# A two-layer transformer pair on one core: the low halves of the mixing stage's split weights, formed by VectorE or by accumulating DMAs

## The chip, the cores and the metric

The kernel runs on one core of a Trainium2 chip. The metric is device time in microseconds (us) of one execution. Before the change three runs took 1903.65, 1903.70 and 1907.62 us, a median of 1903.7 us.

## The reference

256 rows of 1024 numbers pass through a first network of two layers, then a second of two layers. A layer of the first network is

```python
mod = silu(c) @ ada_w[l] + ada_b[l]                      # nine vectors: shift, scale, gate x 3
h = h + 0.5 * g1 * swiglu(modulate(rms_norm(h), sh1, sc1), ffn1_w_in[l], ffn1_w_out[l])
z = modulate(rms_norm(h), sh2, sc2) @ w_in[l]            # 1024 -> 2564 columns: the mixing part
mixed = concat(diff_attention(z), conformer_conv(z), spatial_gating(z), forgetting_attention(z))
h = h + g2 * (mixed @ w_out[l])
h = h + 0.5 * g3 * swiglu(modulate(rms_norm(h), sh3, sc3), ffn2_w_in[l], ffn2_w_out[l])
```

The convolution is causal and depthwise, 31 taps wide. The second network (attention with three kinds of heads, then an MLP) is not touched by the change.

## The kernel before

**Split products.** Most products are made at full precision from float32r operands, which hold fewer bits than float32. A weight tile `raw` is split into `hi`, its rounded copy, and `lo = raw - hi`; the rows on the other side are split alike. A product is then three matmuls: rows hi by weight hi, rows hi by weight lo, rows lo by weight hi. In `pump` (line 413) ScalarE (ACT) writes `hi` by a copy that rounds (a CAST in the trace) and VectorE (DVE) writes `lo` by a subtraction:

```python
sc_.copy(hi[:, :n], raw[:, :n])
ve.tensor_tensor(lo[:, :n], raw[:, :n], hi[:, :n].bitcast(F), op=OP.subtract)
```

Weights come in chunks of at most 128 x 1024 numbers (512 KB). `fetch` (line 395) loads them through SyncE's queue (SP), in the order of a list `stream`; `pump` makes the splits when its plan finds buffers and time; `chunk` (line 452) hands them to the matmul loops. All large tiles come from one ring of 40 buffers.

**The mixing part** (`mixing`, line 1069) multiplies by `w_in` in six blocks of columns (`MIX_BLOCKS`), each made of four chunks, over two halves of the rows, tt0 and tt1. Blocks 0, 1, 2 and 4 are split: 16 chunks a layer, twelve of 128 x 1024 and the four of block 1 of 128 x 520. I number them 0 to 15 in the order of use. Blocks 3 and 5 and all of `w_out` stay whole (float32, no split). `gemm_in` (line 791) runs over blocks and halves; where the rows of tt1 are not ready it takes block 0 tt0, block 1 tt0, block 0 tt1, block 1 tt1. Block 0 feeds the convolution, whose 31 taps for two column halves run on DVE (`conv`, line 1113), block 1 and 2 the forgetting attention, 3 and 5 the differential attention, 4 the spatial gating.

**Rows.** Before the mixing part `Normed` (line 597) takes each half's sum of squares on ACT (two `junk` instructions, one for each 512 columns), the reciprocal root on GpSimd (POOL), scales the rows on DVE, and `to_xT` (line 700) transposes them on TensorE (PE) into two banks, applies the modulation (the first bank on ACT, the second on DVE; `c<-bank,mod,mod` in the trace) and splits them. The residual sums of the stage before (`ev<-bank,c`, then `h<-h,ev`) are on DVE.

**Order.** Python code records every instruction while it keeps a plan of each engine's clock from costs of its own (`Plan`, `Engine.cost`). Work that isn't a matmul of the main loops is a generator that is stepped when that plan says that it is due. So each engine's program is one fixed sequence, in the order in which the plan met the work, and it waits in that order on the chip. All compute instructions are issued by one helper, line 183, so tiles tell the work apart: `c` is a tile of the ring, `bank` a PSUM bank, `ev`, `sm`, `dl`, `st` smaller tiles.

Of the kernel before, what the change touches and what calls it, by code (L numbers as in the profile page):

```python
# [7 lines left out]
F = mybir.dt.float32  # L8
R = mybir.dt.float32r
AF = mybir.ActivationFunctionType  # L10
OP = mybir.AluOpType
AX = mybir.AxisListType

P = 128
# [12 lines left out]
MIX_BLOCKS = [[(768, 512)], [(2304, 260)], [(1792, 512)], [(0, 512)], [(1280, 512)], [(512, 256)]]  # L27
# [8 lines left out]
def width(block):  # L36
    return sum(n for _, n in block)


def in_sizes(blocks):  # L40
    return [2 * width(b) for b in blocks for _ in range(4)]


def out_sizes(k):
    return [1024] * (k // P)
# [197 lines left out]
def two_blocks(ctx: ExitStack, tc, w, out, dbg=None, stages=99):  # L243
    nc = tc.nc
    pool = ctx.enter_context(tc.tile_pool(name="sb", bufs=1))
# [9 lines left out]
    WHOLE = (3, 5)  # L255
    plan = Plan()
    pe, ve, sc_, gp = (Engine(plan, k, e) for k, e in (("pe", nc.tensor), ("dve", nc.vector), ("act", nc.scalar), ("pool", nc.gpsimd)))
# [36 lines left out]
    def wait(cond, what):  # L294
        n = 0
        while not cond():
            pump()
            if not bg.tick():
                bg.idle()
            flush()  # L300
            n += 1
            assert n < 20000, (what, st, arena.free, psr.free, mine, smr.free, dlr.free, evr.free, describe())
# [11 lines left out]
    def drain(entries):  # L314
        n = 0
        while True:
            left = [e for e in entries if e[2] is not None]
            if not left:
                return
            pump()  # L320
            moved = bg.tick()
            for e in left:
                if e[2] is bg.rest and e not in bg.rest[: bg.width] and e[1] <= plan.now:
                    moved += bg.step(e)
            if not moved:
                bg.idle()
            flush()
            n += 1
            assert n < 20000, (st, plan.clock, arena.free, psr.free, mine, smr.free, dlr.free, evr.free, describe(), [e[1] for e in bg.urgent + bg.rest])


    units = []

    def add(nm, l, sizes, whole=lambda i: False):
        at = 0
        for i, n in enumerate(sizes):
            units.append((w[nm][l, at * P:(at + n) * P].rearrange("(p n) -> p n", p=P), n, "whole" if whole(i) else None))
            at += n

    parts = []  # L340
    for l in range(L):
        for i in range(3):
            at = len(units)
            if i == 1:
                add("w_in", l, in_sizes(MIX_BLOCKS), lambda i: i // 4 in WHOLE)
                add("w_out", l, out_sizes(D), lambda i: True)
            else:
                add(f"ffn{i // 2 + 1}_w_in", l, in_sizes(FFN_BLOCKS))
                add(f"ffn{i // 2 + 1}_w_out", l, out_sizes(DFF))
            parts.append(units[at:])  # L350
    units.clear()
    for l in range(L):
        at = len(units)
# [37 lines left out]
    def spare(n=1):  # L391

        return arena.free >= n and (st["held"] + n <= NBASE or arena.free >= n + SPARE)

    def fetch():
        while st["fetch"] < len(stream) and st["raws"] < NRAW and spare():
            ap, n = stream[st["fetch"]][:2]
            t = arena.take([P, 1024])
            nc.sync.dma_start(t[:, :n], ap)
            begin = max(plan.clock["dma"], plan.now)  # L400
            plan.clock["dma"] = begin + n * 1.42e-3
            plan.wrote(t, plan.clock["dma"] + 2.0, "dma")
            raw_of[st["fetch"]] = t
            st["fetch"] += 1
            st["raws"] += 1
            st["held"] += 1

    def next_raw():
        del raw_of[st["conv"]]
        st["conv"] += 1  # L410
        st["raws"] -= 1

    def pump(force=False, most=None, goal=None):
        while True:
            fetch()
            i = st["conv"]
            if i >= st["fetch"] or i == most or st["made"] == goal:
                return
            ap, n, what = stream[i]
            raw = raw_of[i]  # L420
            ahead = st["made"] - st["want"]
            if not force and (st["made"] < 4 * EARLY or plan.ready(raw) > plan.now + 0.3):
                return
            if what == "whole":
                chunks.append((raw, None))
                st["made"] += 1
                next_raw()
                continue
            if what is not None:
                if not ada_unit(raw, *what):  # L430
                    return
                arena.put()
                st["held"] -= 1
                next_raw()
                continue
            if st["made"] - st["released"] >= NMOST or not (spare(2) or (force and ahead <= 0 and arena.free >= 2)):
                return
            if not force and st["hurry"] and ahead >= 4:
                return
            late = max(plan.clock["act"], plan.clock["dve"]) - plan.now  # L440
            if not force and late > (0.5 if ahead >= 5 else 2.0 if ahead >= 3 else 4.0):
                return
            hi, lo = arena.take([P, 1024], R), arena.take([P, 1024], R)
            st["held"] += 1
            arena.put()
            sc_.copy(hi[:, :n], raw[:, :n])
            ve.tensor_tensor(lo[:, :n], raw[:, :n], hi[:, :n].bitcast(F), op=OP.subtract)
            chunks.append((hi, lo))
            st["made"] += 1
            next_raw()  # L450

    def chunk():
        i = st["want"]
        n = 0
        while len(chunks) <= i:
            pump(True, goal=min(i + 2, 4 * EARLY) if EARLY <= i < 4 * EARLY else i + 1 if i < EARLY else None)
            if len(chunks) <= i and not bg.tick():
                bg.idle()
            flush()
            n += 1  # L460
            assert n < 20000, (st, arena.free, describe())
        st["want"] += 1
        c = chunks[i]
        chunks[i] = None
        return c
# [75 lines left out]
    def ada_unit(raw, l, v, kt):  # L541
        key = (l, v)
        if v % 3 != 2:
            t = mod_tile(l, v)
            ve.tensor_tensor_reduce(raw, raw, cond_row, scale=1.0, scalar=K("ada_b", 72 * l + 8 * v + kt, 1), op0=OP.mult, op1=OP.add,
                                    accum_out=t[:, kt:kt + 1])
            if kt + 1 in (FIRST if key in ((0, 0), (0, 1)) else [KT]):
                a = slice(mod_there[key], kt + 1)
                if v % 3 == 1:
                    ve.scalar_tensor_tensor(t[:, a], t[:, a], 1.0, K("norm_g", 24 * l + 8 * (v // 3) + a.start, a.stop - a.start),  # L550
                                            op0=OP.add, op1=OP.mult)
                mod_there[key] = a.stop
            return True
        if key not in ada_acc:
            if not room(3):
                return False
            ada_acc[key] = arena.take([P, D]), arena.take([P, D])
            br = ada_acc[key][1]
            nc.sync.dma_start(br[0:1], w["ada_b"][l:l + 1, v * D:(v + 1) * D])
            plan.wrote(br, plan.now + 3.0, "dma")  # L560
        acc, br = ada_acc[key]
        c = cond[:, kt:kt + 1]
        if kt == 0:
            ve.tensor_scalar(acc, raw, c, None, op0=OP.mult)
        else:
            ve.scalar_tensor_tensor(acc, raw, c, acc, op0=OP.mult, op1=OP.add)
        if kt == KT - 1:
            ve.tensor_tensor(acc[0:1], acc[0:1], br[0:1], op=OP.add)
            arena.put()
            bg.add(ada_reduce(l, v, acc), urgent=True, due=plan.ready(acc) + 2.0)  # L570
        return True
# [1073 lines left out]
    at = CON["causal"][0]  # L1645
# [166 lines left out]
```

## Time and profile before

| | |
|---|---|
| runs | 1903.65, 1903.70, 1907.62 us |
| the profiled execution's own time | 1907.24 us |
| its span on the core | 1905.5 us, mean granted TensorE clock 0.996 |
| PE busy | 1864.3 us (98%), 8672 matmuls |
| DVE busy | 1303.6 us (68%), 2044 instructions |
| ACT busy | 972.5 us (51%), 1506 instructions |
| POOL busy | 17.0 us (1%), 56 instructions |
| DMA | 397.32 MB, mean 209 GB/s |

A busy PE is not a PE at its peak: matmuls are pipelined and their ends are modelled. In the rows below a group or a timeline row gives engine, operation, output tile and input tiles, shapes and count; what stands in square brackets is how long the engine sat idle before it and what ended that. PEclk is the granted TensorE clock as a share of full speed. The mixing parts of the two layers lie at about 195 to 330 us and 690 to 825 us of the span.

### The profile page before, as it was taken

How to read it: one execution, taken by the hardware profiler on the slowest of the kernel's cores; microseconds unless marked ns; L12 is line 12 of the kernel's file. 1: busy time of each engine (PE TensorE's matmuls, PEld its weight loads, DVE VectorE, ACT ScalarE, POOL GpSimd, SP SyncE). 2: the span in 40 equal slices, each digit the busy share in tenths (PEclk: the TensorE clock that was granted, in tenths of full speed). 3: DMA queues.
4: the chain of work that ended last, by engine and by line, in shares of the span. 5: the costliest groups of instructions: out<-in, count | busy, mean ns of one | idle time of the engine just before them, and what ended most of it. 6: DMA issues, size and time to landing. Idle time of an engine off the chain costs nothing.

```text
span 1905.5 us, 23848 instructions
## 1 busy us (share of the span) xinstructions
PE 1864.3 (98%) x8672; PEld 1487.9 (78%) x8672; DVE 1303.6 (68%) x2044; ACT 972.5 (51%) x1506; POOL 17.0 (1%) x56
## 2 busy tenths in 40 slices
PE   6999999999999999999999999999999999999998
PEld 5788864888888886668888787888888787888886
DVE  7999796878697967865566646676654546666561
ACT  5544545444454545654445646555543645645460
POOL 0000000000000000000000000000000000000000
PEclk9999999999999999999999999999999999999999
DMA  9989752678688865435565343655574343654460
GB/s 384 382 329 394 259 192 78 234 268 297 246 296 288 334 240 194 156 130 189 192 239 188 111 155 102 215 170 167 180 250 141 125 159 107 197 195 160 146 220 34
DMA packets 110579, 397.32 MB, mean 209 GB/s; under 512 B 12278, under 2 KB 12406, under 8 KB 110460
## 3 DMA queue, kind: packets, MB, share of 16 engines
q1 hardware_dynamic: 109020, 391.88, 59.4%
q10 hardware_dynamic: 1440, 3.91, 0.6%
q8 instruction: 68, 1.11, 0.2%
q14 instruction: 51, 0.42, 0.1%
HBM read 394.69 MB, written 1.05 MB: 208 GB/s over the span
## 4 chain that ended last, share of the span: by engine, by line
PE 87%; DVE 5%; ACT 5%; issue 1%; DMA 1%; POOL 0%; ACTq 0%; POOLq 0%; DVEq 0%
PE bank L183 87%; DVE c L183 3%; ACT sm L183 2%; ACT c L183 2%; DVE sm L183 1%; ACT L175 1%; DMA cond_row<-in_c_dram 0%; DVE ev L183 0%; DMA c<-in_ada_w_dram 0%; DMA c<-in_w_out_b_dram 0%; DVE st L183 0%; DVE h L183 0%; ACT ev L183 0%; ACT junk L183 0%; ACT dl L183 0%
## 5 line engine op out<-in xcount | busy, mean ns | idle before, releaser
L183 PE MATMUL bank<-c,c 128*128 128x512 f32 (+3 forms) x7392 | 1761.9, 396 | 10.9 <-ACT c L183 7.8
L183 PEld LDWEIGHTS bank<-c,c 128*128 128x128 f32 (+1 forms) x7392 | 1350.0, 188 | 327.4 <-issue 45.8
L183 DVE TENSOR_TENSOR c<-c,c 128x1024 fp32r<-128x1024 f32 (+4 forms) x614 | 711.5, 1182 | 233.4 <-ACT c L183 225.4
L183 ACT CAST c<-c 128x1024 fp32r<-128x1024 f32 (+4 forms) x600 | 592.0, 1025 | 112.7 <-PE bank L183 74.7
L183 ACT ACTIVATE ev<-bank 128x256 f32<-128x256 f32 (+1 forms) x100 | 40.0, 401 | 198.4 <-PE bank L183 196.2
L183 DVE CUSTOM_DVE_ANT_0 c<-c,cond_row,col 128x1024 f32<-128x1024 f32 x96 | 121.9, 1275 | 0.0
L183 ACT CAST c<-bank 128x512 fp32r<-128x512 f32 (+1 forms) x100 | 55.2, 553 | 86.5 <-PE bank L183 86.5
L183 DVE TENSOR_TENSOR c<-bank,c 128x512 fp32r<-128x512 f32 (+2 forms) x108 | 69.6, 647 | 24.1 <-ACT c L183 24.1
L183 DVE TENSOR_TENSOR ev<-ev,bank 128x256 f32<-128x256 f32 x88 | 36.4, 417 | 67.4 <-ACT ev L183 67.1
L183 ACT ACTIVATE ev<-bank,st 128x512 f32<-128x512 f32 x56 | 38.5, 688 | 77.6 <-PE bank L183 77.6
L183 ACT ACTIVATE junk<-h 128x512 f32<-128x512 f32 x44 | 27.8, 631 | 95.2 <-DVE h L183 94.8
L183 PEld LDWEIGHTS bank<-con,ev 128*128 128x128 f32 x432 | 55.9, 140 | 25.5 <-issue 4.9
L183 PE MATMUL bank<-con,ev 128*128 128x128 f32 x432 | 72.3, 273 | 3.2 <-DVE ev L183 3.2
L183 ACT CAST c<-ev 128x512 fp32r<-128x512 f32 x28 | 17.4, 620 | 91.4 <-DVE ev L183 91.2
L183 ACT ACTIVATE c<-bank,st 128x512 f32<-128x512 f32 x36 | 24.8, 688 | 75.2 <-PE bank L183 69.7
L183 DVE SCALAR_TENSOR_TENSOR c<-c,cond,c 128x1024 f32<-128x1024 f32 x42 | 53.7, 1278 | 0.0
L183 DVE TENSOR_TENSOR ev<-ev 128x512 f32<-128x512 f32 x32 | 22.1, 690 | 45.5 <-ACT ev L183 45.5
L183 DVE TENSOR_TENSOR ev<-bank,c 128x512 f32<-128x512 f32 x40 | 27.4, 685 | 34.4 <-PE bank L183 34.3
L183 DVE SCALAR_TENSOR_TENSOR c<-c,col,c 128x256 f32<-128x256 f32 x120 | 48.8, 474 | 0.0
L183 ACT ACTIVATE sm<-sm,st 128x128 f32<-128x128 f32 x72 | 31.8, 443 | 17.3 <-DVE st L183 17.3
L183 DVE TENSOR_TENSOR h<-h,bank 128x512 f32<-128x512 f32 x16 | 10.9, 682 | 42.1 <-PE bank L183 42.1
L183 DVE TENSOR_TENSOR c<-ev,c 128x512 fp32r<-128x512 f32 x28 | 19.4, 692 | 23.1 <-ACT c L183 23.0
(106 smaller groups left out, 676.0 us busy)
## 6 DMA issues: line engine op xcount, KB each, us to landing
c<-in_ffn_w_in_dram SPq DMA_DIRECT2D x176, 512.0 KB, 4.8
c<-in_w_in_dram SPq DMA_DIRECT2D x152, 512.0 KB, 4.2
c<-in_ada_w_dram SPq DMA_DIRECT2D x144, 512.0 KB, 5.9
c<-in_ffn_w_out_dram SPq DMA_DIRECT2D x88, 512.0 KB, 5.5
c<-in_w_up_dram SPq DMA_DIRECT2D x64, 512.0 KB, 4.2
c<-in_w_down_dram SPq DMA_DIRECT2D x64, 512.0 KB, 4.3
c<-in_w_out_dram SPq DMA_DIRECT2D x16, 512.0 KB, 4.4
c<-in_w_o_dram SPq DMA_DIRECT2D x16, 512.0 KB, 4.2
```

Of the source, the lines that this page charges most:

```text
L175: self.eng.preload_act_table_set(table)
L183: return fn(*args, **kw)
```

## The change

For the 32 split chunks of the two mixing parts, ACT writes the negated rounded copy into `lo` (an `ACTIVATE` with scale -1 into a float32r tile), a DMA issued by POOL adds `raw` to it where it lies, and ACT then writes `hi` as before. The subtraction on DVE goes. In the plan's books the DMA takes 1 us of POOL, and `lo` is there 6 us later.

```diff
-    def add(nm, l, sizes, whole=lambda i: False):
+    def add(nm, l, sizes, whole=lambda i: False, other=None):
...
-            units.append((w[nm][l, at * P:(at + n) * P].rearrange("(p n) -> p n", p=P), n, "whole" if whole(i) else None))
+            units.append((w[nm][l, at * P:(at + n) * P].rearrange("(p n) -> p n", p=P), n, "whole" if whole(i) else other))
...
-                add("w_in", l, in_sizes(MIX_BLOCKS), lambda i: i // 4 in WHOLE)
+                add("w_in", l, in_sizes(MIX_BLOCKS), lambda i: i // 4 in WHOLE, "added")
...
-            if what is not None:
+            if what not in (None, "added"):
...
+            if what == "added":
+                sc_.activation(lo[:, :n], raw[:, :n], AF.Copy, scale=-1.0)
+                nc.gpsimd.dma_start(lo[:, :n], raw[:, :n], accum_op=OP.add)
+                plan.note("pool", 1.0, [], [lo, raw])
+                plan.wrote(lo, plan.clock["pool"] + 6.0, "dma")
             sc_.copy(hi[:, :n], raw[:, :n])
-            ve.tensor_tensor(lo[:, :n], raw[:, :n], hi[:, :n].bitcast(F), op=OP.subtract)
+            if what is None:
+                ve.tensor_tensor(lo[:, :n], raw[:, :n], hi[:, :n].bitcast(F), op=OP.subtract)
```

The plan's new costs also move other instructions. Three places in layer 0 show it; layer 1 has the same new order in all three.

**ACT, from the squares of the rows of tt1 (`junk`) to the modulation of those rows (`ACTIVATE c<-bank,mod,mod`).** The CASTs from a `c` tile of 128x520 are chunks of block 1, that of 128x1024 is chunk 8, the first of block 2. Before:

```order
L183 ACTIVATE junk_1931,st_1916<-h_66 128x512
L1080 DMA ws<-in_gmlp_ws_dram 128x512
L1082 DMA c_1943<-in_gmlp_rows_dram 128x512
L183 CAST c_1961<-c_1775 128x520
L183 CAST c_1970<-c_1780 128x520
L183 CAST c_1979<-c_1787 128x520
L175 ACT_TABLE_LOAD
L183 ACTIVATE ev_1988<-bank_1945 128x256
L183 CAST c_1997<-c_1795 128x1024
L183 ACTIVATE c_2005<-bank_2006,mod_3_1006,mod_4_790 128x128 x4
```

Now:

```order
L183 CAST c_1959<-c_1766 128x520
L183 ACTIVATE c_1967<-c_1775 128x520
L183 CAST c_1966<-c_1775 128x520
L183 ACTIVATE c_1980<-c_1780 128x520
L183 CAST c_1979<-c_1780 128x520
L175 ACT_TABLE_LOAD
L183 ACTIVATE ev_1989<-bank_1943 128x256
L183 ACTIVATE c_1999<-c_1787 128x520
L183 CAST c_1998<-c_1787 128x520
L183 ACTIVATE c_2006<-c_1796 128x1024
L183 CAST c_2005<-c_1796 128x1024
L183 ACTIVATE c_2014<-bank_2015,mod_3_1006,mod_4_790 128x128 x4
```

Ahead of the second piece stand the same two DMA issues and chunk 4's ACTIVATE. So between the squares and the modulation ACT now has five chunks twice (four of 520, one of 1024), where it had three of 520 and one of 1024 once.

**DVE, from the first taps of the convolution to the scaled rows `dl` of the forgetting attention's tt0.** The taps are `SCALAR_TENSOR_TENSOR` on a `c` tile of 128x256; `st<-ev` is the reduction that `dl` depends on. Before:

```order
L183 TENSOR_SCALAR c_2167<-c_2040,col 128x256 x2
L183 SCALAR_TENSOR_TENSOR c_2167<-c_2040,col,c_2167 128x256 x8
L183 TENSOR_TENSOR ws<-ws,con 128x512
L183 TENSOR_REDUCE st_2206<-ev_2205 128x8
L183 TENSOR_TENSOR c_2222<-c_2001,c_2221 128x1024
L183 SCALAR_TENSOR_TENSOR c_2167<-c_2040,col,c_2167 128x256 x8
L183 TENSOR_TENSOR dl_2203<-bank_2160,st_2242 128x8x64
```

Now:

```order
L183 TENSOR_SCALAR c_2182<-c_2037,col 128x256 x2
L183 SCALAR_TENSOR_TENSOR c_2182<-c_2037,col,c_2182 128x256 x16
L183 TENSOR_TENSOR ws<-ws,con 128x512
L183 TENSOR_REDUCE st_2226<-ev_2225 128x8
L183 SCALAR_TENSOR_TENSOR c_2182<-c_2037,col,c_2182 128x256 x8
L183 TENSOR_TENSOR dl_2223<-bank_2172,st_2250 128x8x64
```

A subtraction of 128x1024 is gone, and 24 taps instead of 16 stand ahead of `dl`.

**PE, the transposes of that `dl` among the matmuls of block 3** (whole weights; `bank_2252` before, `bank_2273` now). Before:

```order
L183 MATMUL bank_2252<-c_1908,c_1867 128x512 x2
L183 MATMUL bank_2252<-c_1965,c_1867 128x512 x2
L183 MATMUL bank_2252<-c_1974,c_1867 128x512
L183 MATMUL bank_2278<-con,dl_2203 65x128 x4
L183 MATMUL bank_2284<-con,dl_2203 65x128 x4
```

Now:

```order
L183 MATMUL bank_2273<-c_1964,c_1871 128x512 x2
L183 MATMUL bank_2290<-con,dl_2223 65x128 x4
L183 MATMUL bank_2296<-con,dl_2223 65x128 x4
L183 MATMUL bank_2273<-c_1971,c_1871 128x512 x2
L183 MATMUL bank_2273<-c_1984,c_1871 128x512 x2
```

The transposes stood behind five matmuls of block 3 and stand behind two. (A float32 matmul of this list is two instructions in the trace.)

## Rows read from the trace of the kernel before

**Rows 1.** The page, parts 1 and 4: busy time of engines; the last chain.

```profile
PE 1864.3 (98%) x8672; PEld 1487.9 (78%) x8672; DVE 1303.6 (68%) x2044; ACT 972.5 (51%) x1506; POOL 17.0 (1%) x56
...
PE 87%; DVE 5%; ACT 5%; issue 1%; DMA 1%; POOL 0%; ACTq 0%; POOLq 0%; DVEq 0%
```

**Rows 2.** Busy time by stretch: length, PE, PEld, DVE, ACT, POOL, PEclk, DMA, GB/s.

```profile
195.00:330.00 135.00, 130.34 (x579) 89.86 (x577) 105.91 (x266) 73.54 (x166) 2.39 (x9) 0.97 0.51 173
690.00:825.00 135.00, 131.25 (x595) 91.47 (x594) 99.61 (x255) 72.99 (x166) 2.44 (x9) 0.99 0.48 160
...
240.00:250.00 10.00, 10.00 (x38) 6.62 (x37) 10.00 (x22) 3.64 (x7) 0.00 (x0) 1.00 0.62 211
```

**Rows 3.** The same view, layer 1, around a wait of PE for block 2.

```profile
736.00:738.00 2.00, 0.50 (x1) 0.19 (x1) 1.23 (x2) 2.00 (x3) 0.00 (x0) 1.00 0.01 2
738.00:740.00 2.00, 1.85 (x5) 1.47 (x6) 2.00 (x5) 0.06 (x1) 0.00 (x0) 0.56 0.00 0
```

**Rows 4.** Groups by form: the subtractions, and an ACTIVATE of 128x1024.

```profile
L183 DVE TENSOR_TENSOR c<-c,c 128x1024 fp32r<-128x1024 f32 x574 | 687.8, 1220 | 228.0 <-ACT c L183 220.6 <-PE bank L183 2.6 <-DMA c<-in_ffn_w_in_dram 2.1
...
L183 ACT ACTIVATE c<-c 128x1024 f32<-128x1024 f32 x12 | 12.0, 1050 | 0.0
...
L183 DVE TENSOR_TENSOR c<-c,c 128x520 fp32r<-128x520 f32 x8 | 5.2, 693 | 0.0
```

**Rows 5.** Timeline (start, us), layer 0: rows of tt0, then tt1, into the mixing part.

```profile
206.05 2.93 ACT L183 CAST c<-c 128x1024 fp32r<-128x1024 f32 x3
...
209.34 1.50 ACT L183 ACTIVATE c<-bank,mod,mod 128x128 f32<-128x128 f32 x4 [0.36 <-PE bank L183]
...
212.14 1.36 DVE L183 TENSOR_SCALAR c<-bank,mod,mod 128x128 f32<-128x128 f32 x4
...
215.41 0.68 DVE L183 TENSOR_TENSOR ev<-bank,c 128x512 f32<-128x512 f32 x1
...
219.15 1.68 ACT L183 CAST c<-c 128x520 fp32r<-128x520 f32 x3 [0.19 <-issue]
...
219.52 0.55 POOL L183 TENSOR_TENSOR st<-st,small 128x1 f32<-128x1 f32 x1
...
220.10 0.76 DVE L183 TENSOR_SCALAR c<-h,st 128x1024 f32<-128x1024 f32 x1 [0.94 <-POOL st L183]
...
223.36 1.51 ACT L183 ACTIVATE c<-bank,mod,mod 128x128 f32<-128x128 f32 x4
...
225.57 8.87 PE L183 MATMUL bank<-c,c 128*128 128x512 f32 x48 [0.54 <-ACT c L183]
```

**Rows 6.** Timeline, layer 0: last copies of block 2, taps, block 2 tt0's end, block 3, `dl`.

```profile
233.49 1.99 ACT L183 CAST c<-c 128x1024 fp32r<-128x1024 f32 x2
...
239.75 3.25 DVE L183 SCALAR_TENSOR_TENSOR c<-c,col,c 128x256 f32<-128x256 f32 x8
240.17 0.60 ACT L183 ACTIVATE ev<-bank 128x512 f32<-128x512 f32 x1 [1.18 <-PE bank L183]
...
245.56 4.54 PE L183 MATMUL bank<-c,c 128*128 128x512 f32 x10
...
249.94 1.04 PE L183 MATMUL bank<-con,dl 128*65 128x128 f32 x8
```

**Rows 7.** Loads of `w_in`: from issue to landing, us.

```profile
DMA to landing us min/median/max: 2.8/4.3/9.0
```

**Rows 8.** Timeline, layer 0: gating reads block 4 tt1; the next stage's first transposes.

```profile
276.31 0.60 ACT L183 ACTIVATE c<-bank 128x512 f32<-128x512 f32 x1 [1.53 <-PE bank L183]
...
330.36 1.06 PE L183 MATMUL bank<-con,c 128*128 128x128 f32 x8
```

**Rows 9.** Timeline, layer 1: copies of block 1; first matmuls after block 4; next transposes.

```profile
716.24 1.69 ACT L183 CAST c<-c 128x520 fp32r<-128x520 f32 x3 [0.18 <-issue]
...
777.09 1.03 PE L183 MATMUL bank<-c,c 128*128 128x256 f32 x4
...
824.35 1.09 PE L183 MATMUL bank<-con,c 128*128 128x128 f32 x8
```

## Prediction, made before the changed kernel ran

> **What bounds the kernel now.** I began with the page's busy times and last chain. TensorE is busy for 98% of the span and holds 87% of the chain that ended last; VectorE, which the change relieves, is busy for 68% and holds 5% [rows 1]. So time taken from VectorE is worth something only where TensorE stands still. The change touches the two mixing parts, so I next read the busy times of those two stretches. TensorE lacks 135 - 130.34 = 4.7 us in layer 0 and 135 - 131.25 = 3.8 us in layer 1, and the granted clock, 0.97 and 0.99, costs some 0.03 x 135 + 0.01 x 135 = 5.4 us more [rows 2]. That is 13.9 us: more than this the change cannot give. The reader should also see that VectorE is full in a stretch such as 240 to 250 us, while TensorE is full there too [rows 2]. Third, the timeline around the places where the weights of the mixing part are split shows which copy each matmul waits for: there ACT, not VectorE, ends TensorE's waits, as at 225.57 us [rows 5].
>
> **What is removed.** 24 subtractions of 1.22 us and 8 of 0.69 us [rows 4], 34.8 us of VectorE, 17.4 us a layer. By the order only those of chunks 12 to 15, 4.9 us a layer, lie among the taps of the convolution; the rest lie before it.
>
> **What is added on ACT.** A negated copy for each chunk. An ACTIVATE of 128x1024 takes 1.05 us [rows 4]; back to back, a copy of 128x1024 costs 2.93 / 3 = 0.98 us and one of 128x520 1.68 / 3 = 0.56 us [rows 5]. The order shows where they queue; I follow layer 0.
>
> Step 1, rows of tt0. Chunks 1 to 3 are copied between the squares and the modulation of tt0. Three more copies let ACT reach the modulation at 206.05 + 6 x 0.98 = 211.9 us instead of 209.34 [rows 5]. VectorE's own modulation stands behind the first bank's subtraction: 211.9 + 1.50 + 0.62 + 0.69 = 214.7 us instead of 212.14. Before, chunk 4's subtraction (0.69) stood between it and the residual sums of tt1; that one is gone. So these start at about 217.4 us instead of 215.41: **+2.0 us**, for all of tt1.
>
> Step 2, rows of tt1. Between squares and modulation ACT now has five more copies of 0.56 us and one of 0.98 us, **+3.8 us**. The modulation moves from 223.36 [rows 5] to 229.2 us, and block 0 tt1 on TensorE, which waited 0.54 us for exactly this chain at 225.57 [rows 5], starts at 231.4 us. Block 1 tt0, the only work put ahead of it, fills little of the gap.
>
> Step 3, block 2. Three more negations (chunks 9 to 11) stand on ACT before the last copy of block 2, which ended at 233.49 + 1.99 = 235.5 us [rows 6]: now 235.5 + 5.8 + 2.9 = 244.2 us, the negation a microsecond earlier, at 243.2. Then the accumulate. No row shows one. The nearest are the loads of as many bytes, 2.8 to 9.0 us from issue to landing [rows 7]. Less than nothing is excluded, since the matmul waits for it. I take the median, 4.3 us: 247.5 us, and 1.1 us of matmuls after it. Block 2 tt0 ends at 248.6 us instead of 240.17 [rows 6], **+8.4 us**.
>
> Step 4, the convolution's place. Its taps start after ACT's copies of step 3: just ahead of the tap row at 239.75 us stand two TENSOR_SCALARs, 0.7 us, so 239.1 + 8.7 = 247.8 us now. Sixteen taps come first, then the mask and the reduction (0.7 us each), eight taps, and the `dl` product: 247.8 + 0.7 + 6.5 + 1.3 + 3.3 + 0.6 = 260.2 us, by the tap row's 3.25 us for eight [rows 6]. TensorE is there at 248.6 + 5.2 (block 2 tt1) + 1.7 (two matmuls of block 3; 4.54 us for five of them [rows 6]) = 255.5 us and waits. It transposed `dl` at 249.94 us [rows 6] with five of those matmuls done, so the loss is 260.3 - 249.9 + 3 x 0.9 = **12.9 us**. The subtraction that stood here is already left out; with it the wait would be 1.2 us longer.
>
> Step 5, what is paid back. From here on VectorE is ahead and TensorE runs on. Block 4 ends at 276.2 + 12.9 = 289.1 us. From its end to the next stage's transposes TensorE took 330.36 - 276.2 = 54.1 us in layer 0 [rows 8], with waits and a low clock, but 824.35 - 777.09 = 47.3 us in layer 1 [rows 9]. With the convolution ready early I give both layers 47. Layer 0: 336.1 us, **+5.8 us**. Layer 1 stands at the same place of ACT's order 716.24 - 219.15 = 497.1 us later [rows 5, 9], and its new order is the same: 289.1 + 497.1 + 47 = 833.2 us against 824.35 [rows 9], **+8.9 us**. It loses more because its old order had less to pay back.
>
> **POOL and SP.** POOL was busy for 17 us [rows 1], so its 32 issues find it free; each waits for its negation, and the reciprocal roots of the rows (one ended at 220.07 us [rows 5]) stand between them in the order. The accumulates that those roots wait behind have their negations done on ACT before the squares, so the roots lose nothing. Loads that reuse a `raw` buffer wait for its accumulate; they are issued far ahead, and I cost that at nothing. If that cover is gone, one landing time a layer is lost.
>
> **Sum.** 5.8 + 8.9 = 14.7 us. The profiled execution's own time is 1907.2 us, so 1921.9 us by it; it lies 3.5 us above the median of the runs, and from that, 1903.7 us, I forecast **1918 us**.
>
> **A page against the rows.** The loads took 2.8 to 9.0 us [rows 7]. The Trainium skill, "DMA: Bandwidth & Descriptors", section "Anatomy of one DMA — SWDGE (gpsimd) path", gives a DMA issued by GpSimd about 2.0 us plus its bytes at 436 GB/s; for 512 KB I work out 3.2 us, an estimate from that page. By it step 3 would be 1.1 us shorter and the sum the same, since step 4 waits for VectorE either way; no row here shows such a DMA.
>
> **The rivals.** (a) *VectorE's relief wins, faster.* All that the mixing parts can give is 13.9 us [rows 2]. For it: VectorE full at 240 to 250 us. It decides if ACT's added copies find idle time, that is, if chunks are split earlier than the order suggests. Against it: the wait at 225.57 us names ACT [rows 5]. Half of it: 1897 us.
>
> (b) *No change.* The delays of steps 1 to 4 are there, and the last third of the stage, where layer 0 lost 54.1 - 47.3 = 6.8 us, pays back more than I give it in both layers: 1906 us.
>
> (c) *Late landing.* The accumulate of chunk 4 is issued after the root of tt1, at 220.1 + 2.0 = 222.1 us, and by the order the transposes of tt1 (1.0 us) stand behind its first use on TensorE. ACT reaches the modulation at 229.2 us, so from 229.2 - 1.0 - 222.1 = 6.1 us of landing on, each further microsecond delays both layers. At 9.0 us: 2 x 2.9 = 5.8 us, 1924 us; an accumulate that reads two operands may need longer, 1930 us at 12 us. VectorE's scaling of the rows follows the same root and holds VectorE for 0.76 us, for 1024 columns in which a subtraction takes 1.22 us [rows 4, 5]. If POOL cannot issue beside it, landings longer than 5.3 us are enough. That is what the Trainium skill's page "SBUF — State Buffer", section "Who interferes with whom", leads one to expect: it says that a VectorE instruction in a two-port mode locks GpSimd out, and that this starves the descriptors of a GpSimd DMA. No row here shows an issue by POOL to weigh it by.
>
> Low clock belongs to all of them: after a slice in which TensorE worked 0.5 of 2 us the grant was 0.56 [rows 3]. The waits of steps 2 to 4 are as long, but most of what then runs slowly waits for ACT anyway; I add nothing, and up to 3 us a layer to the upper end.
>
> **How the numbers follow.** Forecast 0.57, its own range 1911 to 1925; (c) 0.18; (b) 0.14; (a) 0.11. About 0.2%, 3.8 us, is what a measurement can tell from no change. Faster by more: (a), 0.11. Within: (b) but for 0.01, so 0.13. Slower: 0.57 + 0.18 + 0.01 = 0.76. The range of 8 in 10 leaves out (a) and the far end of (c): 1903 to 1931 us.
>
> **What would show it.** Right: block 0 tt1 waits for ACT some 6 us later after the squares than before; a wait of PE on VectorE before the `dl` transposes; VectorE ending the taps before block 4 ends; both stages longer, layer 1 more. Wrong: PE without new waits between 215 and 262 us; accumulates landing after 6 us or more (then c); the last third still taking 54 us.

## The result, and the profile after

The changed kernel took 1934.9 us (median of 4 runs, 1933.2 to 1936.6) beside 1904.0 us for the one before on the same chip: a ratio of 1.0156, 95% interval 1.0142 to 1.0169, so 31 us slower. I had forecast 1918 us, 14 us slower, and a range up to 1931.

The page of the changed kernel: busy times, two DMA queues (packets, MB, share of 16 engines), the last chain, the costliest group.

```profile
PE 1873.8 (97%) x8672; PEld 1498.8 (77%) x8672; DVE 1270.9 (66%) x2010; ACT 1005.1 (52%) x1544; POOL 45.4 (2%) x88
...
q1 hardware_dynamic: 109020, 391.88, 58.0%
q0 software_dynamic: 4608, 14.71, 4.1%
...
PE 88%; ACT 5%; DVE 3%; DMA 3%; issue 1%; POOL 0%; ACTq 0%; POOLq 0%; DVEq 0%
...
L183 PE MATMUL bank<-c,c 128*128 128x512 f32 (+2 forms) x7392 | 1767.3, 397 | 32.3 <-DMA c<-c 23.4
```

Beside [rows 1], VectorE lost 32.7 us, ACT gained as much, and VectorE's share of the chain fell from 5% to 3%. The last line has the new item: TensorE waited 23.4 us for `DMA c<-c`, the accumulates. Their queue, q0, moved 14.71 MB in 4.1% of the engines' time.

Busy time by stretch, the columns of [rows 2]:

```profile
195.00:330.00 135.00, 119.54 (x544) 88.73 (x543) 82.65 (x238) 84.99 (x177) 15.95 (x23) 0.92 0.77 222
690.00:825.00 135.00, 121.65 (x563) 94.68 (x562) 77.19 (x223) 79.22 (x162) 15.86 (x23) 0.94 0.78 226
246.00:256.00 10.00, 3.69 (x14) 2.44 (x15) 7.84 (x21) 2.00 (x5) 0.01 (x1) 1.00 0.95 267
258.00:260.00 2.00, 2.00 (x6) 1.61 (x5) 2.00 (x6) 0.51 (x2) 0.00 (x0) 0.50 0.00 0
```

TensorE lacks 15.5 and 13.4 us instead of 4.7 and 3.8, and the clock fell to 0.92 and 0.94. (Over the whole stages, which now end later, it lacks as much: 15.5 of 150.7 us and 13.4 of 149.5.) Between 246 and 256 us it worked 3.7 of 10 us while the DMA engines were 95% busy, and from 258 to 260 us, behind these waits, the granted clock was 0.50, the lower of its two levels.

TensorE's timeline in layer 0, from the rows of tt1 to the next stage (start, us):

```profile
228.90 0.80 PE L183 MATMUL bank<-c,c 128*128 128x260 f32 x2 [6.20 <-DMA c<-c]
...
246.86 1.65 PE L183 MATMUL bank<-c,c 128*128 128x512 f32 x6 [1.08 <-DMA c<-c]
251.97 1.66 PE L183 MATMUL bank<-c,c 128*128 128x512 f32 x6 [3.46 <-DMA c<-c]
255.62 7.13 PE L183 MATMUL bank<-c,c 128*128 128x512 f32 x23 [1.99 <-DMA c<-c]
...
265.90 1.04 PE L183 MATMUL bank<-con,dl 128*65 128x128 f32 x8
...
295.64 0.60 PE L183 MATMUL bank<-c,c 128*128 128x256 f32 x2
...
300.68 2.24 PE L183 MATMUL bank<-c 32*128 32x256 f32 x14 [1.29 <-DVE c L183]
...
345.71 1.06 PE L183 MATMUL bank<-con,c 128*128 128x128 f32 x8
```

Chunk 4 held TensorE for 6.2 us, the last three chunks of block 2 for 1.1, 3.5 and 2.0. The transposes of `dl`, before which I expected a wait for VectorE, start at 265.90 us with no wait. Block 4 ended at 295.64 us, and the next stage's transposes came 15.4 us later than at 330.36 [rows 8]. ACT's rows that answer to steps 1 to 3 (both modulations, block 2 tt0's end):

```profile
211.93 1.49 ACT L183 ACTIVATE c<-bank,mod,mod 128x128 f32<-128x128 f32 x4
230.59 1.50 ACT L183 ACTIVATE c<-bank,mod,mod 128x128 f32<-128x128 f32 x4 [1.60 <-PE bank L183]
257.08 0.60 ACT L183 ACTIVATE ev<-bank 128x512 f32<-128x512 f32 x1 [8.79 <-PE bank L183]
```

Layer 1, TensorE (the first four answer to the waits above, then block 4's end and the next stage):

```profile
740.61 0.80 PE L183 MATMUL bank<-c,c 128*128 128x260 f32 x2 [5.51 <-DMA c<-c]
...
758.68 1.65 PE L183 MATMUL bank<-c,c 128*128 128x512 f32 x6 [1.19 <-DMA c<-c]
762.46 1.65 PE L183 MATMUL bank<-c,c 128*128 128x512 f32 x6 [2.13 <-DMA c<-c]
...
765.98 5.54 PE L183 MATMUL bank<-c,c 128*128 128x512 f32 x23 [1.86 <-DMA c<-c]
...
804.41 0.60 PE L183 MATMUL bank<-c,c 128*128 128x256 f32 x2
...
854.47 1.06 PE L183 MATMUL bank<-con,c 128*128 128x128 f32 x8
```

Against 824.35 [rows 9] that is +30.1 us: 15.35 from layer 0 and 14.77 of its own. Both spans, 1934.8 and 1905.5, differ by 29.3, so everything happened in the two mixing parts. All 32 accumulates together, from issue to landing:

```profile
DMA to landing us min/median/max: 3.6/6.8/10.6
```

I had put 4.3 us there, the median of the loads [rows 7]. By size, the page's medians are 7.3 us for the 24 accumulates of 512 KB and 6.4 us for the 8 of 260 KB (block 1).

### The profile page after: what moved, and what is told of

It is laid out like the page before. It is cut to its first block, busy times and chain, and to the rows that moved or that the text cites. A ratio compares the mean times of both kernels' runs of the same rounds, so it can differ in the third digit from the quotient of the medians.

```text
span 1934.8 us, 23947 instructions
## 1 busy us (share of the span) xinstructions
PE 1873.8 (97%) x8672; PEld 1498.8 (77%) x8672; DVE 1270.9 (66%) x2010; ACT 1005.1 (52%) x1544; POOL 45.4 (2%) x88
## 3 DMA queue, kind: packets, MB, share of 16 engines
q0 software_dynamic: 4608, 14.71, 4.1%
## 4 chain that ended last, share of the span: by engine, by line
PE 88%; ACT 5%; DVE 3%; DMA 3%; issue 1%; POOL 0%; ACTq 0%; POOLq 0%; DVEq 0%
PE bank L183 88%; ACT c L183 2%; DVE c L183 2%; DMA c<-c 2%; ACT sm L183 1%; ACT L175 1%; DMA c<-in_ffn_w_in_dram 1%; DMA cond_row<-in_c_dram 0%; DVE ev L183 0%; DVE h L183 0%; DVE sm L183 0%; DMA c<-in_w_out_b_dram 0%; ACT junk L183 0%; POOL st L183 0%; ACT dl L183 0%
## 5 line engine op out<-in xcount | busy, mean ns | idle before, releaser
L183 PE MATMUL bank<-c,c 128*128 128x512 f32 (+2 forms) x7392 | 1767.3, 397 | 32.3 <-DMA c<-c 23.4
L183 PEld LDWEIGHTS bank<-c,c 128*128 128x128 f32 x7392 | 1355.7, 189 | 351.4 <-issue 48.0
L183 DVE TENSOR_TENSOR c<-c,c 128x1024 fp32r<-128x1024 f32 (+4 forms) x582 | 677.7, 1188 | 249.4 <-ACT c L183 239.7
L183 ACT ACTIVATE c<-c 128x1024 fp32r<-128x1024 f32 (+2 forms) x44 | 42.2, 974 | 0.5 <-issue 0.5
```

Of the source, the lines that this page charges most:

```text
L183: return fn(*args, **kw)
```

## The experiments

My first theory (A) was that the late landings make the difference; rivals were ACT's added copies (B) and the new order (C). Ratios are to the kernel before, each run beside it on its own chip.

### The four parts of the loss

**The order alone.**

```diff
-                sc_.activation(lo[:, :n], raw[:, :n], AF.Copy, scale=-1.0)
-                nc.gpsimd.dma_start(lo[:, :n], raw[:, :n], accum_op=OP.add)
+                plan.note("act", 0.05 + 0.88 * n / 1000, [lo[:, :n]], [raw[:, :n]])
...
+            if what == "added":
+                nc.vector.tensor_tensor(lo[:, :n], raw[:, :n], hi[:, :n].bitcast(F), op=OP.subtract)
```

> The changed order of every engine, but with the instructions of before: VectorE's subtraction is back, the negated copy and the accumulate are gone (the plan still books them). Theory A (late landing: the accumulates land 7 us after their issue where I counted 4.3, and TensorE waits) and theory B (the 32 added copies on ACT) both expect about the time of before, 1900 to 1910 us, since neither is there. Theory C (the new order is itself bad) expects 1920 us or more.

Measured: 1.0038 (1.0023 to 1.0053), 7 us. None of the three hit: the order costs something of its own, less than C said.

**Without the accumulates.**

```diff
-                nc.gpsimd.dma_start(lo[:, :n], raw[:, :n], accum_op=OP.add)
```

> The changed kernel without the accumulating DMA: lo holds the negated copy alone, so the low part is left out of the result. ACT's added copies and the order stay. Theory A expects most of the 31 us gone, 1908 to 1918 us, with TensorE's wait for chunk 4 of some 6 us a layer ended by ACT some 3 us earlier at most. Theory B expects 1925 us or more. Theory C expects 1925 us or more here and in the run of the order alone.

Measured: 1.0106 (1.0090 to 1.0121), 1925.9 us. That is B's number: only about 9 us of the 31 went. Its TensorE timeline:

```profile
230.87 7.44 PE L183 MATMUL bank<-c,c 128*128 128x512 f32 x36 [0.22 <-ACT c L183]
...
258.65 1.06 PE L183 MATMUL bank<-con,dl 128*65 128x128 f32 x8 [3.54 <-DVE dl L183]
...
288.42 0.60 PE L183 MATMUL bank<-c,c 128*128 128x256 f32 x2
...
338.48 1.06 PE L183 MATMUL bank<-con,c 128*128 128x128 f32 x8
```

This is the path of my steps 1 to 4, and the wait for VectorE before `dl` that I had foreseen is there: 3.54 us. Layer 1's own transposes stood at 843.69 us, 19.3 later than before.

**Copies and subtraction.** The same, with VectorE's subtraction written over the negated copy.

```diff
-                nc.gpsimd.dma_start(lo[:, :n], raw[:, :n], accum_op=OP.add)
...
+            if what == "added":
+                nc.vector.tensor_tensor(lo[:, :n], raw[:, :n], hi[:, :n].bitcast(F), op=OP.subtract)
```

> The changed order with ACT's negated copies and, in place of the accumulate, VectorE's subtraction, which overwrites the negated copy: nothing is relieved. Against the run without the accumulates (1925.9 us) this prices VectorE's relief. TensorE waited there 3.5 us a layer for VectorE's scaled rows and 2.6 and 2.1 us for its sums, so I expect the relief to be worth 4 to 10 us: 1930 to 1936 us. If VectorE's work is hidden, 1924 to 1928 us.

Measured: 1.0117 (1.0102 to 1.0133), 1928.8 us, below what I expected. The two intervals overlap: relieving VectorE of 34.8 us is worth at most a few us. From the order alone to here, ACT's added copies cost 0.0117 - 0.0038 = 0.0079, 15 us.

**A plain copy in the accumulate's place.**

```diff
-                nc.gpsimd.dma_start(lo[:, :n], raw[:, :n], accum_op=OP.add)
+                nc.gpsimd.dma_start(lo[:, :n], raw[:, :n])
```

> The changed kernel with the DMA copying raw over lo without adding, so that lo holds the whole weight and not its low part; same bytes, same queue, same order. Theory A1 (any DMA of POOL's that goes from one place on the chip to another lands late among the loads) expects 1928 to 1937 us and a median landing of 6 us or more for 512 KB. Theory A2 (the addition makes it slow: its DMA engines take 1.9 times as long per byte as those of the loads) expects a median of 4 to 5 us and 1912 to 1924 us.

Measured: 1.0111 (1.0096 to 1.0126), 1927.2 us, as without any DMA: the landings of A2 (4.6 us in the median for 512 KB), but a time between the two ranges, 3 us above A2's and 1 us below A1's, since the copies and the order stay. All its landings, and its queue's line:

```profile
DMA to landing us min/median/max: 2.3/4.1/7.2
```

```profile
q0 software_dynamic: 4608, 14.71, 2.2%
```

Packets and bytes are the same as in the changed kernel, the engines' time is 2.2% instead of 4.1%: adding costs 1.9 times as much, and nearly all of the landing's 9 us hangs on that. My own 4.3 us fits a plain copy.

### Whether the parts add up

**`hi` on VectorE**, so that ACT has one copy a chunk, at the same places of the order.

```diff
-            sc_.copy(hi[:, :n], raw[:, :n])
+            if what == "added":
+                plan.note("act", 0.05 + 0.88 * n / 1000, [hi[:, :n]], [raw[:, :n]])
+                nc.vector.tensor_copy(hi[:, :n], raw[:, :n])
+            else:
+                sc_.copy(hi[:, :n], raw[:, :n])
```

> The changed kernel, order and accumulates kept, with the rounded copy hi of the 32 chunks written by VectorE, so that ACT has one copy a chunk as before. If ACT's doubled copies cost the 13 to 16 us that the runs without the accumulates say, 1920 to 1927 us, unless the copies on VectorE (about 0.7 us each if like its other one-input operations) delay something else. If they don't matter, 1932 us or more.

Measured: 1.0166 (1.0150 to 1.0183), no gain. GpSimd issued chunk 4's accumulate 1.5 us earlier, and TensorE came no earlier (first GpSimd, then TensorE):

```profile
220.61 2.77 POOL L448 DMA_DIRECT2D c<-c  x3 [0.23 <-issue]
```

```profile
228.90 0.80 PE L183 MATMUL bank<-c,c 128*128 128x260 f32 x2 [6.53 <-DMA c<-c]
```

The landings grew instead, to 8.5 us in the median and 12.0 at most, and GpSimd's issues to 1.02 us in the median and 2.24 at most. So this run takes ACT's second copies away, but it does not hold the landings as they were.

**Neither.** The same with the accumulates left out as well.

> The changed order with neither the accumulates nor ACT's doubled copies: hi on VectorE, the negated copy on ACT, no DMA (the low part is left out of the result). Taking away the copies alone won nothing (1937.6 us), taking away the accumulates alone won 9 us (1925.9 us). If the two hold up the same matmuls, so that either alone is enough, both away give much more than the sum of the two: 1908 to 1916 us, about the time of the order alone. If they add up, 1924 to 1929 us.

Measured: 1.0018 (1.0009 to 1.0028), 1908.7 us. So the two hold up the same matmuls:

| changed order | ACT copies twice | ACT copies once |
|---|---|---|
| accumulates | 1.0156 | 1.0166 |
| none | 1.0106 | 1.0018 |

With the accumulates there, taking ACT's second copy away gains nothing, though the later landings may have a part in that; without them it gains 0.9%, even though VectorE has the copy instead. Theory A by itself fell, and so did B: each is enough to hold the same matmuls up, and taking away one alone hides what it is worth.

### Why an accumulate lands late

**Nine DMAs behind the last work**, when no load is in flight.

```diff
...
+    nc.gpsimd.dma_start(x[0], h[0], accum_op=OP.add)
...
+    nc.gpsimd.dma_start(x[0], h[0])
...
+    nc.gpsimd.dma_start(x[1], h[0], accum_op=OP.add)
+    nc.gpsimd.dma_start(x[2], h[0], accum_op=OP.add)
+    nc.gpsimd.dma_start(x[3], h[0], accum_op=OP.add)
```

> The changed kernel with nine more DMAs of 512 KB behind its last work, when no load is in flight: three accumulates one after another, two plain copies, one accumulate, then three accumulates at once. If an accumulate is slow of itself, it lands in 6 us or more here too. If it is the loads beside it that make it late, an accumulate alone lands in 3.5 to 4.5 us and a plain copy in 2.3 to 3 us. Of the four at the end that may overlap, the fourth is issued only when the first has landed if the queue holds three. The time itself says nothing: it has the nine DMAs on top.

The timeline's GpSimd rows: a lone accumulate, two plain copies, then four accumulates on four tiles.

```profile
1937.87 0.89 POOL L1717 DMA_DIRECT2D c<-h  x1 [4.08 <-DMA c<-h]
...
1947.73 0.57 POOL L1719 DMA_DIRECT2D c<-h  x1 [4.01 <-DMA c<-h]
1951.04 0.54 POOL L1720 DMA_DIRECT2D c<-h  x1 [2.75 <-DMA c<-h]
1954.36 0.88 POOL L1721 DMA_DIRECT2D c<-h  x1 [2.77 <-DMA c<-h]
1955.08 1.07 POOL L1722 DMA_DIRECT2D c<-h  x1
1955.94 1.10 POOL L1723 DMA_DIRECT2D c<-h  x1
1959.29 0.86 POOL L1724 DMA_DIRECT2D c<-h  x1 [2.24 <-issue]
```

Alone, an accumulate of 512 KB landed in 4.6 us and a plain copy in 2.9; of the four together the first landed in 4.6, the next in 6.5 and 8.3, the last, issued later, in 7.6. The lone one lies between the two cases, near that of the loads. Stretches of that run (last two columns: DMA share, GB/s), first during an accumulate, then a plain copy, then several accumulates:

```profile
1940.00:1941.00 1.00, 0.00 (x0) 0.00 (x0) 0.00 (x0) 0.00 (x0) 0.00 (x0) 0.50 1.06 201
...
1949.00:1950.00 1.00, 0.00 (x0) 0.00 (x0) 0.00 (x0) 0.00 (x0) 0.00 (x0) 0.50 1.12 410
...
1958.00:1959.00 1.00, 0.00 (x0) 0.00 (x0) 0.00 (x0) 0.00 (x0) 0.00 (x0) 0.50 1.06 197
```

So 4.6 of the 7.3 us of a 512 KB accumulate belong to itself. All engines are full at half the rate, so accumulates queue behind each other; the rest, up to 10.6 us, comes where loads are in flight as well. No run took the loads away, but the changed kernel's trace shows them at work. The accumulates' queue (packets, MB, share of the engines), first from 224 to 226 us, then from 226 to 228:

```profile
q0 software_dynamic: 22, 0.05, 12.3%
```

```profile
q0 software_dynamic: 194, 0.37, 102.2%
```

A lone accumulate, issued at 1937.87 us, had the engines 82% busy from 1939 to 1940. Chunk 4's, issued at 222.11, had 12% of them from 224 to 226 us, while the loads' queues had 92%; from 226 us on its queue had them all. So chunk 4 landed late behind loads. In the run with `hi` on VectorE the accumulates had 13% in the same two microseconds: the earlier issue won nothing. At block 2, from 247 to 252 us, the accumulates' queue held 87% and the loads' 20%: there the accumulates mostly stood in each other's way. The Trainium skill, "Collectives: The Full Stack", section "The bandwidth ceiling: the fold count and why AG ≠ RS ≠ AR", says of the add in a collective's reduce step that it is slower because it needs two source reads, with a measured ratio of 1.93; the size agrees here, 4.1% against 2.2%, but the page speaks of collectives, and no run here shows the reason.

**More room for GpSimd's descriptors.** In layer 0 GpSimd stood idle for 4.1 us before the fourth issue after the rows of tt1 (chunk 7), which came just behind chunk 4's landing, 2.6 us after ACT had written its copy (226.6 us):

```profile
222.11 1.91 POOL L448 DMA_DIRECT2D c<-c  x2
224.21 0.85 POOL L448 DMA_DIRECT2D c<-c  x1 [0.19 <-issue]
229.17 0.87 POOL L448 DMA_DIRECT2D c<-c  x1 [4.11 <-issue]
```

```diff
-    nc = _bacc.Bacc("TRN2", target_bir_lowering=False, num_devices=1, dynamic_dma_scratch_size=1024)
+    nc = _bacc.Bacc("TRN2", target_bir_lowering=False, num_devices=1, dynamic_dma_scratch_size=4096)
```

> The changed kernel with four times the space for the descriptors of GpSimd's DMAs. In layer 0 the issue for chunk 7 came 0.3 us after chunk 4 had landed, 4.1 us late, as if the queue held three. If that space is the limit, the issue comes at about 225.3 us and TensorE waits less for block 1: 1928 to 1934 us. If it is not, or if the wait for chunk 4 hides it, no difference: 1933 to 1937 us.

Measured: 1.0159 (1.0144 to 1.0174), no difference, though the issue now came as soon as ACT had written the copy:

```profile
227.42 0.85 POOL L448 DMA_DIRECT2D c<-c  x1 [1.88 <-ACT c L183]
```

So the queue holds three at the old size, which also the fourth of the four above shows, and the limit cost nothing that shows: chunk 4 landed at 228.9 us here too, since the engines are full anyway (a share of 1.03 to 1.13 from 220 to 228 us in the changed kernel).

### The order

**The old order with the accumulates.**

```diff
-                sc_.activation(lo[:, :n], raw[:, :n], AF.Copy, scale=-1.0)
-                nc.gpsimd.dma_start(lo[:, :n], raw[:, :n], accum_op=OP.add)
-                plan.note("pool", 1.0, [], [lo, raw])
-                plan.wrote(lo, plan.clock["pool"] + 6.0, "dma")
+                nc.scalar.activation(lo[:, :n], raw[:, :n], AF.Copy, scale=-1.0)
+                nc.gpsimd.dma_start(lo[:, :n], raw[:, :n], accum_op=OP.add)
...
+                plan.note("dve", 0.07 + 1.04 * n / 1000, [lo[:, :n]], [raw[:, :n], hi[:, :n]])
```

> The instructions of the change in the order of before: the plan books the subtraction on VectorE, the chip gets the negated copy and the accumulate. Theory A expects 1930 to 1950 us, since no other work is put ahead of the first use of a late chunk. Theory B expects 1925 to 1935 us. Theory C (the order is at fault) expects 1915 us or less.

Measured: 1.0205 (1.0183 to 1.0228), 1944.7 us, as theory A said. For accumulates the new order is the better one, by some 9 us.

**A later landing in the plan.**

```diff
-                plan.wrote(lo, plan.clock["pool"] + 6.0, "dma")
+                plan.wrote(lo, plan.clock["pool"] + 12.0, "dma")
```

> The changed kernel with the plan told that an accumulate lands after 12 us instead of 6. If the loss by landing is there because the plan put first uses too early, TensorE's waits for accumulates fall from 23 us to under 10 us in both layers and the time to 1922 to 1930 us. If there is no other work to put ahead, the waits stay and it takes 1932 us or more.

Measured: 1.0306 (1.0288 to 1.0324), 1965.6 us, the worst of all. TensorE's waits for accumulates did fall, from 23.4 to 7.9 + 8.2 = 16.1 us, not below the 10 us that I had asked for, and what the plan put ahead made new ones, for VectorE (8.3 us in layer 0 up to 300 us, where the changed kernel has 0.4): `dl` was transposed 7.1 us later than in the changed kernel, and the next stage began 13.6 us later. Layer 0's waits of TensorE, from 195 to 300 us (total, times, longest):

```profile
PE bank L183 <- DMA c<-c: 7.9, 4, 3.1
PE bank L183 <- DVE c L183: 4.7, 2, 3.6
PE bank L183 <- DVE ev L183: 3.6, 2, 3.3
```

**Filling the wait in the last third.** Three matmuls (six instructions) ahead of the score matmuls at 300.68 us.

```diff
...
+            for _ in range(warm if not banks else 0):
+                nc.tensor.matmul(ps[:, :384], ident, C("dil")[:, :384], start=True, stop=True)
             pe.matmul(ps[:, :P], qT[:, :P], kT[:, :P], start=True, stop=True)
...
```

> The changed kernel with three more matmuls of 128x384 ahead of the first score matmuls of the differential attention in each layer, where TensorE waited 1.29 us for VectorE and then ran 8 to 10 us at half clock; their sums are overwritten. If that wait is what takes the clock down, the clock stays up and the last third goes from 50.1 to 46 to 48 us a layer: 1926 to 1931 us. If the small score matmuls themselves take it down, or if what runs at half clock there waits for VectorE anyway, the last third stays at 50 us: 1933 to 1938 us.

Measured: 1.0162 (1.0148 to 1.0176), no gain. The stretch from 300 us, of the changed kernel and then of this run:

```profile
300.00:312.00 12.00, 11.32 (x44) 8.23 (x45) 11.62 (x56) 6.35 (x29) 0.00 (x0) 0.57 0.07 28
```

```profile
300.00:312.00 12.00, 10.60 (x68) 7.44 (x64) 9.29 (x44) 7.86 (x29) 0.00 (x0) 1.00 0.27 93
```

The clock did stay up, 1.00 instead of 0.57, and the last third shrank from 50.1 to 48.0 us in layer 0 and 49.5 in layer 1, but not to 47, since VectorE now ends other waits there, the longest:

```profile
312.14 0.44 PE L183 MATMUL bank<-con,ev 128*128 128x128 f32 x2 [1.54 <-DVE ev L183]
```

These 2.6 us in two layers do not show in the time. In this profile TensorE's clock around the waits for block 2, from 246 to 256 us, was 0.63 instead of 1.00, and block 4 had ended 2.4 us later, at 298.04 us, before the first of the new matmuls. So what the fill is worth by itself stays open.

### Tries for a faster kernel

**Block 4 alone**, with the plan's own order and then in the order of before (the edit of the old order above).

```diff
...
-                add("w_in", l, in_sizes(MIX_BLOCKS), lambda i: i // 4 in WHOLE, "added")
+                add("w_in", l, in_sizes(MIX_BLOCKS), lambda i: i // 4 in WHOLE, lambda i: "added" if i // 4 == 4 else None)
```

> Only block 4 (chunks 12 to 15 of each layer) by negated copy and accumulate; blocks 0, 1 and 2 subtract on VectorE as before. In the changed kernel TensorE never waited for these four accumulates, so theory A (what costs is landings just ahead of their use) expects none of the 9 us of landing and 4 added copies a layer in a stretch where ACT is half idle: 1898 to 1908 us. If the order that the plan makes is what costs (7 us in the run of the order alone, 3 us a layer of it in the last third of the stage), 1908 to 1915 us.

> Block 4 alone by copy and accumulate, in the order of before (the plan books VectorE's subtraction). If its landings are covered there, VectorE's relief of 4.9 us a layer comes without a new order: 1900 to 1906 us. If they are not (the run of all chunks in the old order waited 2.2 us for one of them), 1906 to 1914 us.

Measured: 1.0032 (1.0019 to 1.0045), as the case of the plan's order said, and 1.0011 (1.0001 to 1.0021), 1907.0 us, no difference that counts, at the near end of the case of landings that are not covered. Even with four chunks TensorE waited for one of them in layer 0, 0.9 us in the first run and 1.3 in the second, and the relief of VectorE gave nothing back.

**The subtraction on GpSimd.**

```diff
...
-            if what is None:
-                ve.tensor_tensor(lo[:, :n], raw[:, :n], hi[:, :n].bitcast(F), op=OP.subtract)
+            (gp if what == "added" else ve).tensor_tensor(lo[:, :n], raw[:, :n], hi[:, :n].bitcast(F), op=OP.subtract)
```

> No negated copy and no DMA: GpSimd, nearly idle, subtracts for the 32 chunks instead of VectorE (the plan books 2.1 us for 1024 columns). If VectorE's relief is worth something and GpSimd's subtraction takes 3 us or less, 1896 to 1908 us. If it takes 5 us or more, or stands in VectorE's way, it is late as the accumulates were: 1915 to 1935 us.

Measured: 1.0173 (1.0158 to 1.0188), 1939.6 us, beyond both cases. GpSimd's group and, in layer 0, VectorE's scaling of the rows, first of tt0, then of tt1:

```profile
L183 POOL TENSOR_TENSOR c<-c,c 128x1024 fp32r<-128x1024 f32 x24 | 61.2, 2567 | 395.4 <-ACT c L183 221.8 <-PE bank L183 159.9 <-issue 12.4
```

```profile
212.16 2.86 DVE L183 TENSOR_SCALAR c<-h,st 128x1024 f32<-128x1024 f32 x1 [0.95 <-POOL st L183]
...
227.90 1.77 DVE L183 TENSOR_SCALAR c<-h,st 128x1024 f32<-128x1024 f32 x1 [0.95 <-POOL st L183]
```

GpSimd needs 2.57 us, under the 3 us that I had asked for, but VectorE's row scaling takes 2.86 us beside a subtraction of 128x1024 and 1.77 beside one of 128x520 (1.41 us), instead of 0.76 [rows 5]. That is what the Trainium skill's page "SBUF — State Buffer", section "Who interferes with whom", says of the two engines: where a VectorE instruction in a two-port mode meets one of GpSimd's, whichever issues first holds the shared pair of ports for its whole instruction. TensorE's waits in layer 0 then name VectorE (14.4 us) much more than GpSimd (2.0 us).

**Filling waits in the kernel before**: six matmuls of 128x256 in layer 0's last third.

```diff
+            for _ in range(3 if l == 0 and p == 0 else 0):
+                nc.tensor.matmul(o[:, :S], ident, C("dil")[:, :S], start=True, stop=True)
...
+            for _ in range(3 if l == 0 else 0):
+                nc.tensor.matmul(bank[:, 0:2].rearrange("p a b c -> p (a b c)"), ident, C("dil")[:, :256], start=True, stop=True)
```

> The kernel before the change with six more matmuls of 128x256 in layer 0's last third, ahead of the gating's row product and of the differential attention's value product, where TensorE stood idle 1.15 and 1.38 us and then ran 7 us at half clock. If filling the waits keeps the clock up, 1 to 4 us faster than before; if the work there waits for VectorE and ACT anyway, no difference or a microsecond slower.

Measured: 1.0004 (0.9995 to 1.0012), no difference, with the clock at 1.00 where it had been 0.57 (304 to 312 us). No version beat the kernel before.

## Why the prediction was right and wrong

The sign was right, and so were most of its steps; the size was half. The table sets its milestones (us) beside the run without accumulates and the changed kernel.

| | predicted | no accumulates | changed |
|---|---|---|---|
| layer 0: modulation of tt1 on ACT | 229.2 | 228.7 | 230.6 |
| `dl` transposes | 260.3 | 258.7 | 265.9 |
| block 4's end | 289.1 | 288.4 | 295.6 |
| last third | 47 | 50.1 | 50.1 |
| next transposes | 336.1 | 338.5 | 345.7 |
| loss of layer 0 | 5.8 | 8.1 | 15.4 |
| loss of layer 1 | 8.9 | 11.2 | 14.8 |

**Steps 1 and 2 were right.** The modulation of tt0 came at 211.93 us for 211.9, that of tt1 at 228.7 without accumulates for 229.2. The cost of ACT's queue came out of counting copies between two places of its order.

**Step 3 failed, by the landing.** I wrote "I take the median, 4.3 us", from loads. Measured were 7.3 us in the median for 512 KB: an accumulate alone takes 4.6, and it meets loads and other accumulates on full engines. Of block 2's last three the landings, from GpSimd's issues at 239.55, 243.12 and 245.02 us to TensorE's starts at 246.86, 251.97 and 255.62, were up to 7.3, 8.9 and 10.6 us. Block 2 tt0 ended at 257.1 us instead of 248.6.

**Step 4 was right as far as it went.** The wait for VectorE, 3.54 us and the transposes at 258.7 for 260.3, is there without accumulates. With them it is covered: VectorE wrote `dl` from 261.48 us, and TensorE was held by the late chunks until 255.6 and came to the transposes at 265.9. My remark that a shorter landing would leave the sum the same was right for the same reason; I did not turn it round and ask from which landing on block 2 decides. By the predicted times TensorE would have waited 260.3 - 255.5 = 4.8 us, so from 4.3 + 4.8 = 9.1 us on for the last chunk. It took up to 10.6, from an issue 1.8 us later than the 243.2 us at which I had its negation done. By its own terms the loss in this step is 10.4 + 2.7 = 13.1 us, not 12.9; what follows from it is 0.2 us a layer too low.

**Step 5 failed, by 3.1 us a layer.** I took 47 us, layer 1's old order. In the changed kernel and seven of the runs in its order the last third took 50.1 to 50.2 us in 14 of 16 layers, with or without accumulates and copies. The two others, where the clock stayed higher (0.89 from 280 to 312 us with neither cause, where the changed kernel had 0.84; 1.00 from 788 to 822 us with the larger descriptor space, against 0.85), took 48.4 and 48.0. So the half clock behind TensorE's wait is worth up to 2 us (0.6 in layer 1 of the run with the fill); the rest is the new order's waiting for VectorE, which is argued from where the waits moved and was not tried by itself.

**The sum.** 14.7 predicted, plus 6.1 for step 5, less 1.4 for steps 1 to 4 (block 4 ended 0.7 us earlier than predicted in each layer by itself) makes 19.4; the run without accumulates has 19.3. The landing adds 10.8 by the two profiles (9.5 by the ratios): 30.1.

**The rivals.** (a) fell: VectorE's relief is worth at most a few us. (b) fell: the last third gave layer 0 back 4.0 us (54.1 to 50.1) and cost layer 1 another 2.8. (c) was the right mechanism, at the place that it named: chunk 4 took 6.8 us from 222.11, more than the threshold of 6.1, and delayed the modulation by 1.4 us, of which 0.7 is the landing beyond the threshold and the rest the transposes behind it, which took 1.91 us instead of 1.0 at a granted clock of 0.50 (228 to 232 us). But it named only this place; most of the price lay at block 2, where I gave the landing no rival. Of GpSimd being locked out by VectorE's row scaling little showed: the two issues beside it took 1.91 us, where one takes 0.87 in the median.

**Low clock.** I added nothing for it behind the waits of steps 2 to 4, and that was too little. In layer 0 the clock fell to 0.50 from 258 to 260 us, and the 23 instructions behind block 2's last landing took 7.13 us; in layer 1 it stayed at 1.00 there and they took 5.54. So some 1.6 us of what the landing cost layer 0 is clock.

**POOL and SP.** "32 issues find it free" was wrong once a layer, by the queue of three, and cost nothing that shows. The loads did wait for accumulates, 100.9 us in 16 waits of SyncE's queue, but none of TensorE's waits in the mixing parts names a load, so costing that at nothing was right.

## What to carry to other kernels

Price a new kind of transfer by both of its numbers, how long one takes from issue to landing and how long it fills the engines, and ask of every place where it is used from which landing time that place decides. Two delays that meet at the same matmuls must be taken away together before either is judged: each of them alone looked worth 0 or 9 us here, both together 26. And an earlier issue brought no earlier landing here while loads filled the engines. Lastly, moving work off an engine that ends few waits buys little, however full it is.

## What the runs showed of the hardware

- An accumulating DMA from one place on the chip to another ran at 197 to 217 GB/s in the microseconds in which all 16 engines were full, a plain one at 410; a lone one of 512 KB landed in 4.6 us against 2.9.
- While loads held 92% of the engines (224 to 226 us), accumulates issued at 222 us had 12%; from 226 us on they had them all.
- GpSimd needs about 0.87 us to issue an accumulate and 0.53 us for a plain copy of the same shape.
- GpSimd's queue took three such DMAs; a fourth issue waited for the first landing, until the space for descriptors was made larger.
- A subtraction of 128x1024 takes GpSimd 2.57 us, and VectorE's row scaling beside it took 2.86 us instead of 0.76.
